# A decoder layer on one core: the mixing written out in set order, weight sums of two leading pairs made earlier, half of the embedding moved beside the first norm

## The chip, the cores and the metric

The kernel runs on one core of one Trainium2 chip. The time is device microseconds of one execution; the kernel before has 2464.32 us as the median of three (2461.43 to 2470.61). TensorE does the matmuls, VectorE (DVE in rows) and ScalarE (ACT) the elementwise work, GpSimd (POOL) the sums of weights, SyncE (SP) issues the transfers. In the trace a matmul's row covers its way through the pipeline; two rows that follow each other start closer together than one is long.

## The reference

One layer and the last norm, for 1024 tokens of width 1024, all in float32:

```
x += 0.5 * (silu(h @ w1) * (h @ w3)) @ w2,  h = rms(x)              # FFN1, inner width 2816
h  = rms(x); q, f, v, og, pool, ga, gb = split(h @ w_in)
f  = lb + (1 - lb) * sigmoid(f);  k = 1 - f;  q = silu(q)            # 8 heads of 128
S_t = diag(f_t) S_{t-1} + k_t outer v_t;  o_t = S_t^T q_t            # chunkwise
y_a = (rms(o) * onorm * silu(og)) @ w_branch_a
y_b = ((trailing means of pool over 2, 4, 8, 16 tokens - token) @ pool_w * scale) @ w_branch_b
x += (sigmoid(ga) * y_a + sigmoid(gb) * y_b) @ w_out
x += 0.5 * SwiGLU_2(rms(x))                                          # FFN2
x += sigmoid(rms(x) @ W_gate) * rms(p @ W_ple);  out = rms(x)
```

## The kernel before, in words

**Products.** Every float32 operand is split into a high and a low part, and each product is three matmuls of 128x128 by 128x512 (`mm3`, lines 150 to 152). The projections run in *pairs*: two blocks of 128 weight columns and the two token halves make a 2x2 product in seven multiplications instead of eight (`pair`), 12 matmuls each, 84 for a pair. For them, sums of the weights (S1 to S4) are made on GpSimd (lines 90 and 93), cast to their high parts on ScalarE (118), and the low parts taken on VectorE (119); sums of the activations (T1 to T3, N4) are made once in each norm.

**A norm's start.** Before FFN1, the mixing and FFN2 the first token half is normed and transposed (`first`), then the second half (`second`): TensorE scales and turns a block (L242), VectorE and ScalarE make the sums and their parts for blocks 0 to 3 (`act_second`, lines 191 to 193). Products 1 and 2 of a pair need the first half alone, so three *leading pairs* run these beside `second`; their weight sums are made later. Their further products wait for each of the four blocks in turn: T1's high part is `xT1h`.

**The mixing.** For each of 8 heads and 2 token halves `hgrn` does: diagonal scores (L810), transposes of v (L817), seven levels of scores (L837; each is followed by a masked copy on VectorE, L840, and a multiply of q and k, L87, that the next level's matmuls need), then the state (L863, L867), the output (L885, L887), a norm of it on ScalarE, GpSimd and VectorE (L892), and transposes of the result (L898) that are multiplied with the gate og (L899) and stored. A list `others` holds ten pairs (gates, pool branch); after each head's two halves the program text takes one or two, beside the next head's q and f pair. Where instructions stand on each engine is decided by a scheduler that goes by the text's order as priority.

**Around it.** The pool branch (`pool_group`) makes trailing means on VectorE in doubling steps, in two 512-wide buffers a step. After the heads come `branch_b` (8 column blocks, 24 matmuls each), `branch_a`, `w_out` in token-major form (`tok`), FFN2, the gate of the per-layer embedding (again `tok`) and the last norm. SBUF is in five tag pools: "a" 28, "w" 12 and "q" 4 buffers of 1024 columns, "u" 8 and "h" 5 of 512; PSUM has banks pA (3), pB (1), pC (1), aux (3). Transfers are all issued from one queue of SyncE in the order in which they stand there.

Of the kernel before, what the change touches and what calls it, by code (L numbers as in the profile page):

```python
# [16 lines left out]
P = 128  # L17
# [20 lines left out]
def hybrid_block(ctx: ExitStack, tc: tile.TileContext, a: dict, out: bass.AP):  # L38
# [208 lines left out]
    def norm_act(x, which, tr="aux"):  # L247
# [20 lines left out]
        def second():  # L268
            ts = range(4, 8)
            diag = scales(x, ts)  # L270
            yield
            for kc in range(0, KC, 2):
                p12 = turned_by(x, ts, diag, kc)
# [5 lines left out]
                yield  # L279
# [9 lines left out]

    def flush():  # L290
        while waiting:
            waiting.pop(0)()

    def pair(wa, wb, act, tiles, on11, on22, on21, on12, early=False):
# [6 lines left out]
        def product(i, ps, start):  # L301
            s, b = SIDES[i]
            hi, lo = w[s]
            for k in range(4):
                c = slice(k * P, (k + 1) * P)
                mm3(ps, hi[:, c], lo[:, c], *act[b][k], start and k == 0, k == 3)

# [13 lines left out]
        ra = raw(wa, "ra")  # L321
        if not early:
            rb = raw(wb, "rb")
        w["A11"], w["A12"] = halves(hilo(ra, "w", "wa"))
        if not early:
            sums(ra, rb)
        yield
# [6 lines left out]
        yield  # L334
        if early:
            sums(raw(wa, "ra"), raw(wb, "rb"))
        yield
        flush()
        pb = bank("pB")
        product(6, pa, False)  # L340
        nc.scalar.copy(c2, pa)  # L341
        product(5, pb, True)
        product(7, pa, False)
# [4 lines left out]
        def rest():  # L348
            product(4, pa, False)
            on21(pa)  # L350
            product(3, pb, False)
# [5 lines left out]
    def steps(it, n=9):  # L357
        for _ in range(n):
            if next(it, 0) == 0:
# [5 lines left out]
    def run_pair(*args, **kw):  # L365
        if not starts:
            steps(pair(*args, **kw))
            return

        second, n = starts[0], len(leads)  # L370
        it = pair(*args, **kw, early=True)
        leads.append(it)
        steps(it, 1 if n == 1 else 2)
        if n == 1:

            steps(leads[0], 1)
# [44 lines left out]
    def ffn_up(act, w1, w3, gs, after=None):  # L421
        chunk = []

        def one(c):
# [13 lines left out]
            run_pair(  # L438
# [748 lines left out]
```

## Time and profile before

| what | value |
|---|---|
| median of three (range) | 2464.32 us (2461.43 to 2470.61) |
| the profiled execution's own time, span of its trace | 2467.48 us, 2465.8 us |
| TensorE busy | 2346.3 us (95%), 11003 instructions |
| VectorE / ScalarE / GpSimd busy | 1482.6 (60%) / 975.2 (40%) / 446.4 us (18%) |
| mean granted clock of TensorE over the span | 0.979 |
| transfers | 334.10 MB, mean 135 GB/s |

The share of busy time is a mean over stages with different limits; the granted clock is told as a share of full speed.

### The profile page before, as it was taken

What the parts mean: (1) busy time and instruction counts of PE and PEld (TensorE: products, weight loads), DVE (VectorE), ACT (ScalarE), POOL (GpSimd) and SP (SyncE); (2) the same over time, 40 slices, a digit from 0 to 9 for tenths busy, and PEclk for the clock granted to TensorE, in tenths of its full rate; (3) what the DMA queues carried; (4) which work ended last, traced back from release to release, by engine and by line L of the source; (5) the groups of instructions that cost most, each with busy time, mean ns of one, the idle gap of its engine ahead of it and who ended that gap; (6) DMA issues with size and microseconds to landing.
All of it is one profiled execution on the core that took longest, in us unless ns stands there. A gap on an engine that the chain in (4) does not pass through costs nothing.

```text
span 2465.8 us, 29423 instructions
## 1 busy us (share of the span) xinstructions
PE 2346.3 (95%) x11003; PEld 1919.4 (78%) x11003; DVE 1482.6 (60%) x2026; ACT 975.2 (40%) x1511; POOL 446.4 (18%) x390
## 2 busy tenths in 40 slices
PE   8899999999998999989999989999899999999997
PEld 5688788888877778768778767777688888888885
DVE  5745555468565665684564675676645544568558
ACT  7433333333554334243333331236433333334654
POOL 2222232100013112122212201201232222100000
PEclk9999999999999999999999988999999999999998
DMA  5244554574232213122312346663225433663323
GB/s 205 88 160 140 176 179 139 177 277 141 90 121 76 90 48 120 56 98 74 107 59 79 117 149 209 221 219 129 98 90 175 154 124 112 211 246 124 109 101 133
DMA packets 133951, 334.10 MB, mean 135 GB/s; under 512 B 15280, under 2 KB 15792, under 8 KB 133808
## 3 DMA queue, kind: packets, MB, share of 16 engines
q1 hardware_dynamic: 133808, 332.23, 39.1%
q8 instruction: 86, 1.41, 0.2%
q14 instruction: 57, 0.47, 0.1%
HBM read 230.98 MB, written 101.19 MB: 135 GB/s over the span
## 4 chain that ended last, share of the span: by engine, by line
PE 80%; DVE 9%; ACT 3%; issue 3%; POOL 2%; DMA 2%; SPq 0%; DVEq 0%; POOLq 0%; ACTq 0%
PE pA L150 12%; PE pA L151 12%; PE pA L152 12%; PE pB L151 6%; PE pB L150 6%; PE pB L152 6%; PE aux L837 4%; PE pC L151 3%; PE pC L152 3%; PE pC L150 3%; PE aux L151 2%; PE aux L152 2%; PE aux L150 2%; DVE qk L87 1%; DVE tot L87 1%
## 5 line engine op out<-in xcount | busy, mean ns | idle before, releaser
L90 POOL TENSOR_TENSOR s<-rb 128x512 f32<-128x512 f32 x74 | 102.4, 1384 | 736.2 <-PE pA L152 359.7
L119 DVE TENSOR_TENSOR wtl<-rb,wth 128x1024 fp32r<-128x1024 f32 x74 | 90.7, 1225 | 152.2 <-ACT wth L118 151.8
L118 ACT CAST wsh<-s 128x1024 fp32r<-128x1024 f32 x74 | 77.8, 1051 | 231.0 <-POOL s L93 219.5
L93 POOL TENSOR_TENSOR rb<-ra,s 128x512 f32<-128x512 f32 x74 | 96.4, 1303 | 382.0 <-DVE wd L119 382.0
L837 PEld LDWEIGHTS aux<-qk 128*128 128x128 f32 (+1 forms) x896 | 107.2, 189 | 44.8 <-issue 28.2
L118 ACT CAST wth<-rb 128x1024 fp32r<-128x1024 f32 x74 | 77.6, 1048 | 155.4 <-POOL rb L93 155.4
L118 ACT CAST gh<-gr 128x1024 fp32r<-128x1024 f32 x84 | 81.8, 980 | 135.8 <-PE aux L151 86.4
L118 ACT CAST wah<-ra 128x1024 fp32r<-128x1024 f32 x74 | 77.9, 1052 | 134.9 <-PE pC L151 81.3
L837 PE MATMUL aux<-qk 128*128 128x64 f32 (+1 forms) x896 | 114.5, 272 | 17.4 <-DVE qk L87 16.5
L119 DVE TENSOR_TENSOR gl<-gr,gh 128x1024 fp32r<-128x1024 f32 x84 | 94.8, 1132 | 59.8 <-ACT gh L118 59.7
L150 PE MATMUL pA<-xT1h,wsh 128*128 128x512 f32 x280 | 111.9, 400 | 19.8 <-ACT xT1h L118 19.8
L119 DVE TENSOR_TENSOR wsl<-s,wsh 128x1024 fp32r<-128x1024 f32 x74 | 91.0, 1230 | 61.8 <-ACT wsh L118 50.4
L150 PE MATMUL pA<-xT3h,wth 128*128 128x512 f32 x296 | 118.1, 399 | 4.2 <-ACT g L341 3.2
L150 PE MATMUL pB<-xT1h,wsh 128*128 128x512 f32 x296 | 117.1, 396 | 1.8 <-ACT xT1h L118 0.9
L150 PE MATMUL pC<-x0h,wah 128*128 128x512 f32 x296 | 117.0, 395 | 1.5 <-ACT x0h L118 1.3
L152 PE MATMUL pA<-x0h,wal 128*128 128x512 f32 x296 | 116.7, 394 | 1.6 <-DVE wal L119 1.6
L152 PE MATMUL pB<-xT1h,wsl 128*128 128x512 f32 x296 | 117.9, 398 | 0.0
L151 PE MATMUL pC<-x0l,wah 128*128 128x512 f32 x296 | 116.8, 394 | 1.0 <-DVE x0l L119 1.0
L151 PE MATMUL pB<-xT1l,wsh 128*128 128x512 f32 x296 | 117.0, 395 | 0.4 <-DVE xT1l L119 0.4
L150 PE MATMUL pA<-x0h,wah 128*128 128x512 f32 x296 | 117.2, 396 | 0.0
L151 PE MATMUL pA<-xT3l,wth 128*128 128x512 f32 x296 | 117.0, 395 | 0.0
L152 PE MATMUL pA<-xT3h,wtl 128*128 128x512 f32 x296 | 117.0, 395 | 0.0
(338 smaller groups left out, 6580.6 us busy)
## 6 DMA issues: line engine op xcount, KB each, us to landing
ra<-in_ffn_w_dram SPq DMA_DIRECT2D x50, 512.0 KB, 3.7
rb<-in_ffn_w_dram SPq DMA_DIRECT2D x44, 512.0 KB, 4.0
gsS<-gs SPq DMA_DIRECT2D x88, 256.0 KB, 2.1
rB<-in_ffn_w_dram SPq DMA_DIRECT2D x40, 512.0 KB, 6.7
gr<-gsS SPq DMA_DIRECT2D x40, 512.0 KB, 3.5
gsA<-g SPq DMA_DIRECT2D x66, 256.0 KB, 2.0
gr<-gsA SPq DMA_DIRECT2D x30, 512.0 KB, 5.1
ra<-in_w_in_dram SPq DMA_DIRECT2D x29, 512.0 KB, 3.6
```

Source lines behind the costliest of these rows:

```text
L87: nc.vector.tensor_tensor(o, x, y, ALU.mult)
L90: nc.gpsimd.tensor_tensor(o, x, y, ALU.add)
L93: nc.gpsimd.tensor_tensor(o, x, y, ALU.subtract)
L118: nc.scalar.copy(hi, src)
L119: nc.vector.tensor_tensor(lo, src, hi.bitcast(F32), ALU.subtract)
L150: nc.tensor.matmul(ps, ah, bh, start=first, stop=False, **kw)
L151: nc.tensor.matmul(ps, ah, bl, start=False, stop=False, **kw)
L152: nc.tensor.matmul(ps, al, bh, start=False, stop=last, **kw)
L837: nc.tensor.matmul(ps[:m, c, :64], kc[c][:, :m], right, start=True, stop=True)
```

## The change

- **Mixing.** The eight heads are written under a manual schedule for TensorE: `head` runs a head's two halves in groups of matmuls (a `yield` behind each), and `among` deals the parts of other pairs (three matmuls, then a `yield False`) between the groups. A table `more` says which pairs stand beside which head; heads 1, 3 and 5 have the next v, qf and og pairs. Head 7 gets the last two gate pairs and the first block of `branch_b`.
- **Moved.** The transposes of the result, the gate multiply and the store (`turn`) stand two groups into the next half head. v is loaded ahead, og late. The pool means stand beside the next qf pair's parts, in "w" buffers; their maps follow.
- **Pairs.** The first result is copied from pC and pA added to it (it was the other way around). The weights' A parts of leading pairs go to spare "a" buffers, and the first two leading pairs have their sums made ahead of `second`; the third as before. In the mixing the leading pairs are v(0), qf(0), og(0).
- **FFN1's start.** Half of the embedding's product runs inside `second` (before blocks 0 and 2), its copies out of PSUM on ScalarE; raw weights of two leading pairs are loaded first.
- **Rest.** Order of some loads (`behind`), gb and o buffers; the last two items of the closing `tok` are one, so that its last four banks get twelve matmuls in a row each.

```diff
     def pair(wa, wb, act, tiles, on11, on22, on21, on12, lead=False, late=False,
...
-        w["A11"], w["A12"] = halves(hilo(ra, "w", "wa"))
-        if not early:
-            sums(ra, rb)
-        yield
+        w["A11"], w["A12"] = halves(hilo(ra, "a" if lead else "w", "wa"))
+        yield True
+        if not late:
+            sums(ra, raws[1] or raw(wb, "rb"))
+        yield True
         pa, pc = bank("pA"), bank("pC")
-        product(1, pa, True)
-        nc.scalar.copy(c1, pa)
-        product(2, pc, True)
-        add(c1, c1, pc)
+        yield from product(1, pa, True)
+        yield from product(2, pc, True)
+        nc.scalar.copy(c1, pc)
+        add(c1, c1, pa)
...
     def run_pair(*args, raws=(None, None), **kw):
...
+        second = starts.pop()
+        for it in leads:
             steps(it, 1)
+        steps(leads[0], 2)
+        steps(leads[1], 1)
+        steps(second, 2)
+        steps(leads[1], 1)
+        steps(second, 1)
+        steps(leads[2], 2)
         steps(second)
...
+            while means and next(means[0], 0) == 0:
+                means.pop(0)
...
+            both = t_("w", "pw")
+            nxt = [both[:, L], both[:, R]]
...
+        def turn():
+            ps = bank("aux")
+            for p_, a_ in zip(chunks(ps), qc):
+                nc.tensor.transpose(p_, a_, ident)
+            nc.vector.scalar_tensor_tensor(og, ps, onorm[:, h : h + 1], og, ALU.mult, ALU.mult)
+            store(o_dram[h][half], og)
...
+    GROUPS = 2 * 13
...
+            for i, _ in enumerate(hgrn(h, half)):
+                if i == 2 and turns:
+                    turns.pop(0)()
...
+        for i, _ in enumerate(groups, 1):
+            while done * GROUPS < i * n:
+                next(parts, None)
+                done += 1
...
+    more = {
+        0: lambda: (pool_pair(0), beside_means(qf_pair(1)), pool_maps(),
+                    gate_pair(GB, 0, gb_dram)),
+        2: lambda: (pool_pair(2), beside_means(qf_pair(3)), pool_maps(),
+                    gate_pair(GB, 2, gb_dram)),
+        4: lambda: (qf_pair(5), gate_pair(GB, 4, gb_dram), gate_pair(GB, 6, gb_dram)),
+        6: lambda: (qf_pair(7), gate_pair(GA, 0, ga_dram), gate_pair(GA, 2, ga_dram)),
+        7: lambda: around(gate_pair(GA, 4, ga_dram), act_b(), gate_pair(GA, 6, ga_dram), flushed(),
+                          branch_b(0)),
+    }
...
+            among(its, head(h), (74 if h == 7 else 3 * PAIR + 4 * (h in (0, 2))))
...
-    tok([(i, q) for i in ORDER for q in range(2)],
+    tok([(i, q) for i in ORDER for q in range(2)][:-2] + [(4, (0, 1))],
```

The order on TensorE in the second half of head 7, before (L898 turns the first half's result, L810, L817 and L837 are this half's groups, L150 to L152 a pair's matmuls):

```order
L898 MATMUL aux_10647<-ident,qk_9791 128x128 x4
L810 MATMUL aux_10659<-qk_9792 128x128 x4
L817 MATMUL aux_10665<-ident,v_10655 128x128 x4
L837 MATMUL aux_10680<-qk_9792 128x64 x4
L837 MATMUL aux_10687<-qk_9792 128x64 x4
L837 MATMUL aux_10694<-qk_9792 128x64 x4
L837 MATMUL aux_10701<-qk_9792 128x64 x4
L837 MATMUL aux_10708<-qk_9792 128x64 x4
L150 MATMUL pC_11381<-x0h_11226,wah_11360 128x512
L837 MATMUL aux_10715<-qk_9792 128x64 x4
```

The same place in the changed kernel, whose levels are line 898 (157 to 159 are `mm3`'s):

```order
L898 MATMUL aux_10821<-qk_9771 128x64 x4
L157 MATMUL pA_10651<-xT3h_5582,wth_10647 128x512
L158 MATMUL pA_10651<-xT3l_5583,wth_10647 128x512
L159 MATMUL pA_10651<-xT3h_5582,wtl_10648 128x512
L157 MATMUL pA_10651<-xT3h_5641,wth_10647 128x512
L158 MATMUL pA_10651<-xT3l_5642,wth_10647 128x512
L159 MATMUL pA_10651<-xT3h_5641,wtl_10648 128x512
L157 MATMUL pA_10651<-xT3h_5702,wth_10647 128x512
L158 MATMUL pA_10651<-xT3l_5703,wth_10647 128x512
L159 MATMUL pA_10651<-xT3h_5702,wtl_10648 128x512
L898 MATMUL aux_10837<-qk_9771 128x64 x4
```

Where seven levels stood with hardly a matmul between them, nine matmuls of a gate pair now stand between two levels, as in the other heads.

The order on VectorE before, in the pool branch of one group (pw and o are its means and tokens; no head's instruction stands among these):

```order
L758 SCALAR_TENSOR_TENSOR o_7766<-pw_7948,o_7766 128x496
L84 TENSOR_TENSOR o_7766<-pw_7948,o_7766 128x16
L758 SCALAR_TENSOR_TENSOR o_7765<-pw_7949,o_7765 128x512
L81 TENSOR_TENSOR pw_7989<-o_7763 128x511
L119 TENSOR_TENSOR pb_7958<-o_7766,pb_7958 128x512
L119 TENSOR_TENSOR pb_7967<-o_7765,pb_7967 128x512
L749 COPY pw_7989<-o_7763 128x1
L81 TENSOR_TENSOR pw_7990<-o_7764 128x511
```

In the changed kernel the later steps of one group stand between two levels of head 2: ahead of these rows is the multiply of one level, the last row is the next level's masked copy (L902):

```order
L81 TENSOR_TENSOR pw_7670<-pw_7652 128x508
L81 TENSOR_TENSOR pw_7670<-pw_7652 128x4
L87 TENSOR_TENSOR pw_7670<-pw_7670,invc 128x8
L802 SCALAR_TENSOR_TENSOR o_7233<-pw_7670,o_7233 128x504
L84 TENSOR_TENSOR o_7233<-pw_7670,o_7233 128x8
L802 SCALAR_TENSOR_TENSOR o_7234<-pw_7670,o_7234 128x512
L81 TENSOR_TENSOR f_7437<-f_7437,pB_7575 128x512
L119 TENSOR_TENSOR pwhl_7688<-pwr_7686,pwhl_7688 128x512
L119 TENSOR_TENSOR pb_7691<-o_7236,pb_7691 128x512
L718 TENSOR_SCALAR f_7437<-f_7437,lb_126,lb 128x512
L119 TENSOR_TENSOR pb_7700<-o_7235,pb_7700 128x512
L902 COPY_PREDICATED score_5422<-mask_81,aux_7665 128x64x4
```

A step of the means, the multiplies that end it and the low parts for the map now stand in VectorE's queue between one level's multiply and the next level's copy; before, they stood beside other work, in one piece.

The order on GpSimd at FFN2's start, before: the four powers of the norm of tokens 4 to 7 (L231), then the weight sums of a first and a second pair (L90, L93):

```order
L231 TENSOR_TENSOR rs_12722<-rs_12722,mhalf 128x1
L231 TENSOR_TENSOR rs_12731<-rs_12731,mhalf 128x1
L231 TENSOR_TENSOR rs_12740<-rs_12740,mhalf 128x1
L231 TENSOR_TENSOR rs_12749<-rs_12749,mhalf 128x1
L90 TENSOR_TENSOR s_2254_12704<-rb_12702 128x512
L93 TENSOR_TENSOR s_2254_12704<-s_2254_12704,ra_12700 128x512
L93 TENSOR_TENSOR rb_12702<-ra_12700,rb_12702 128x512
L93 TENSOR_TENSOR rb_12702<-ra_12700,s_2254_12704 128x512
L90 TENSOR_TENSOR s_2329_12987<-rb_12985 128x512
L93 TENSOR_TENSOR s_2329_12987<-s_2329_12987,ra_12983 128x512
```

In the changed kernel (the powers are L238):

```order
L93 TENSOR_TENSOR rb_12637<-ra_12619,rb_12637 128x512
L93 TENSOR_TENSOR rb_12637<-ra_12619,s_2212_12639 128x512
L238 TENSOR_TENSOR rs_12704<-rs_12704,mhalf 128x1
L238 TENSOR_TENSOR rs_12713<-rs_12713,mhalf 128x1
L90 TENSOR_TENSOR s_2221_12686<-rb_12684 128x512
L93 TENSOR_TENSOR s_2221_12686<-s_2221_12686,ra_12625 128x512
L93 TENSOR_TENSOR rb_12684<-ra_12625,rb_12684 128x512
L238 TENSOR_TENSOR rs_12722<-rs_12722,mhalf 128x1
L93 TENSOR_TENSOR rb_12684<-ra_12625,s_2221_12686 128x512
L238 TENSOR_TENSOR rs_12731<-rs_12731,mhalf 128x1
L90 TENSOR_TENSOR s_2292_13029<-rb_13027 128x512
```

The sums of two leading pairs now stand among and ahead of the powers, those of the third behind them.

## Rows read from the trace of the kernel before

**Rows 1.** The page: the span, and busy time of two engines

```profile
span 2465.8 us, 29423 instructions
PE 2346.3 (95%) x11003; PEld 1919.4 (78%) x11003; DVE 1482.6 (60%) x2026; ACT 975.2 (40%) x1511; POOL 446.4 (18%) x390
```

**Rows 2.** The view by windows, TensorE: stretch, length, busy (count), granted clock, DMA

```profile
450.00:500.00 50.00, 50.00 (x222) 1.00 0.63 222
800.00:1450.00 650.00, 615.49 (x3357) 1.00 0.27 89
1450.00:1500.00 50.00, 35.55 (x163) 0.66 0.36 117
1456.00:1494.00 38.00, 24.03 (x107) 0.59 0.30 98
1700.00:1750.00 50.00, 39.43 (x179) 0.86 0.29 106
2450.00:2465.80 15.80, 2.58 (x12) 0.70 0.36 133
```

**Rows 3.** TensorE's waits: us in total, times, longest

```profile
PE pA L150 <- ACT xT1h L118: 19.8, 5, 5.9
PE aux L837 <- DVE qk L87: 16.5, 17, 1.4
PE aux L898 <- DVE qk L892: 15.6, 11, 3.5
```

**Rows 4.** Timeline of a level, second half of head 1: start, us, what, idle before

```profile
907.62 1.02 PE L837 MATMUL aux<-qk 128*128 128x64 f32 x8
908.45 0.48 PE L150 MATMUL pC<-x0h,wah 128*128 128x512 f32 x1
908.67 0.44 DVE L840 COPY_PREDICATED score<-mask,aux 128x256 f32<-128x256 uint16 x1 [1.26 <-PE aux L837]
909.01 0.68 DVE L87 TENSOR_TENSOR qk<-qk,tot 128x512 f32<-128x512 f32 x1
909.92 1.00 PE L837 MATMUL aux<-qk 128*128 128x64 f32 x8
```

**Rows 5.** Timeline, a GpSimd sum, a multiply on VectorE, and the level behind them

```profile
884.16 1.47 POOL L93 TENSOR_TENSOR rb<-ra,rb 128x512 f32<-128x512 f32 x1
884.40 1.77 DVE L87 TENSOR_TENSOR qk<-qk,tot 128x512 f32<-128x512 f32 x1
886.23 0.68 PE L837 MATMUL aux<-qk 128*64 128x64 f32 x8 [0.95 <-DVE qk L87]
```

**Rows 6.** Timeline of TensorE, a level in head 7's second half

```profile
1471.87 1.94 PE L837 MATMUL aux<-qk 128*128 128x64 f32 x8 [1.21 <-DVE qk L87]
```

**Rows 7.** Timeline of VectorE inside a group of the pool branch

```profile
1066.13 0.68 DVE L81 TENSOR_TENSOR pw<-o 128x511 f32<-128x511 f32 x1
1066.80 0.68 DVE L81 TENSOR_TENSOR pw<-pw 128x510 f32<-128x510 f32 x1
```

**Rows 8.** The page's costliest groups: a weight's low part on VectorE

```profile
L119 DVE TENSOR_TENSOR wtl<-rb,wth 128x1024 fp32r<-128x1024 f32 x74 | 90.7, 1225 | 152.2 <-ACT wth L118 151.8
```

**Rows 9.** Timeline of the second feed-forward's start: VectorE and TensorE

```profile
1721.09 0.74 DVE L191 SCALAR_TENSOR_TENSOR t<-tr,gains,b 128x512 f32<-128x512 f32 x1
1741.78 1.75 DVE L119 TENSOR_TENSOR x<-b,x 128x512 fp32r<-128x512 f32 x1
1743.45 2.47 DVE L84 TENSOR_TENSOR t<-b,t 128x512 f32<-128x512 f32 x2
1746.33 0.79 PE L150 MATMUL pA<-xT1h,wsh 128*128 128x512 f32 x1 [4.56 <-ACT xT1h L118]
```

**Rows 10.** Timeline of the end: the last matmul, and VectorE behind it

```profile
2452.20 0.39 PE L152 MATMUL pB<-woh,yl 128*128 128x512 f32 x1
2457.40 2.74 DVE L1100 SCALAR_TENSOR_TENSOR x<-x,rs,gain 128x512 f32<-128x512 f32 x4 [0.47 <-POOL rs L162]
2461.13 1.42 DVE L1100 SCALAR_TENSOR_TENSOR x<-x,rs,gain 128x512 f32<-128x512 f32 x2 [0.73 <-POOL rs L162]
```

More of the change, by code (lines that the diff above doesn't have):

```diff
@@ L288, in hybrid_block, with flushed, pair @@
     waiting = []
+    def flushed():
+        while waiting:
+            yield from waiting.pop(0)()
     def flush():
-        while waiting:
-            waiting.pop(0)()
-    def pair(wa, wb, act, tiles, on11, on22, on21, on12, early=False):
+        for _ in flushed():
+            pass
+    def pair(wa, wb, act, tiles, on11, on22, on21, on12, lead=False, late=False,
+             raws=(None, None)):
         c1, c2, c3 = tiles
@@ L357, in steps @@
     def steps(it, n=9):
-        for _ in range(n):
-            if next(it, 0) == 0:
+        for end in it:
+            n -= end
+            if not n:
                 return
@@ L598, in hybrid_block, with embed @@
     e_ss = small("e_ss", [P, NT, 2])
-    def embed(half, ps_):
-        for t in range(4 * half, 4 * half + 4):
+    def embed(ts, ps_, banks):
+        for t in ts:
             c = slice((t % 4) * P, (t % 4 + 1) * P)
             for d in range(2):
-                ps = bank(("pA", "pB")[d])
+                ps = bank(banks[d])
                 for k in range(2):
@@ L713, in done @@
             store(v_dram[h + i][half], t)
-        out_pair(w_in[V + h], w_in[V + h + 1], act, done)
+            v_there.add((h + i, half))
+        yield from out_pair(w_in[V + h], w_in[V + h + 1], act, done)
+    og_there, og_last = set(), [None]
     def og_pair(h):
@@ L726, in done @@
             store(og_dram[h + i][half], t)
-        out_pair(w_in[OG + h], w_in[OG + h + 1], act, done)
+            og_there.add((h + i, half))
+        yield from out_pair(w_in[OG + h], w_in[OG + h + 1], act, done)
     def gate_pair(at, j, dst):
@@ L733, in done, with beside_means, pool_means @@
             store(dst[j + i][half], t)
-        out_pair(w_in[at + j], w_in[at + j + 1], act, done)
-    pw_split = []
-    def pool_group(g, u):
+        yield from out_pair(w_in[at + j], w_in[at + j + 1], act, done)
+    means, pooled = [], []
+    def beside_means(it):
+        for part in it:
+            yield part
+            while means and next(means[0], 0) == 0:
+                means.pop(0)
+        while means:
+            for _ in means.pop(0):
+                pass
+    def pool_means(g, u):
         win = 2 << g
@@ new lines, in among, with around @@
+    def among(its, groups, n):
+        parts = (p for it in its for p in it if not p)
+        done = 0
+        for i, _ in enumerate(groups, 1):
+            while done * GROUPS < i * n:
+                next(parts, None)
+                done += 1
+        for _ in parts:
+            pass
+    PAIR = 28
+    def around(first, acts, *its):
+        yield first
+        next(acts)
+        for it in its[:-1]:
+            yield it
+        next(acts)
+        yield its[-1]
+    more = {
[8 more added lines that the diff above has]
+    }
@@ L934, in branch_b, with act_b @@
+    for it in (v_pair(0), qf_pair(0), og_pair(0)):
+        steps(it)
+    m_parts = []
+    def act_b():
+        behind[0] = latest[0]
+        for g in range(NG):
+            m = t_("q", "m")
+            for half, c in enumerate((L, R)):
+                load(m[:, c], m_dram[g][half])
+            m_parts.append(halves(hilo(m, "a", "m")))
+        m_last, behind[0] = latest[0], None
+        yield True
+        behind[0] = m_last
+        yield True
     def branch_b(j):
@@ L943, in branch_b @@
                 mm3(ps, wh[:, c], wl[:, c], *m_parts[g][half], i == 0, i == 3)
-            t = t_("u", "o")
-            mul(t, ps, gb)
-            store(yb_dram[j][half], t)
+                yield False
+            mul(gb, ps, gb)
+            store(yb_dram[j][half], gb)
+    with tc.manual_schedule(engines={nc.tensor.engine}):
+        for h in range(HEADS):
+            its = more[h]() if h in more else (v_pair(h + 1), qf_pair(h + 1), og_pair(h + 1))
+            among(its, head(h), (74 if h == 7 else 3 * PAIR + 4 * (h in (0, 2))))
+        turns.pop(0)()
+    behind[0] = og_last[0]
     act_a = new_act()
@@ L970, in load_act @@
         put(("T3", "T2"), hilo(b2, "a", "xT3"))
-    for j in range(KC):
-        branch_b(j)
+    for j in range(1, KC):
+        steps(branch_b(j))
         if j % 2:
             load_act(j // 2)
+    behind[0] = latest[0]
     for j in range(0, KC, 2):
```

206 lines of the change are left out of this document (104 added, 102 removed).

## The prediction

> **What bounds it now.** I read the page first: TensorE is busy 2346.3 of 2465.8 us [rows 1], so 119.5 us without a matmul is all that waits can give back, beside what a low clock costs; the number of TensorE instructions hardly changes. The windows say where it lies. In FFN1 a stretch of 50 us is busy 50.00 at a granted clock of 1.00, with 222 matmuls: 0.225 us each, nothing to win there [rows 2]. The seven heads from 800 to 1450 us lose 650 − 615.49 = 34.5 us, the next 50 us lose 14.45, FFN2's start (1700 to 1750) 10.6, the end 15.8 − 2.58 = 13.2 [rows 2]. The waits name the releasers: T1's high part at the starts of the norms 19.8 us in 5 waits, the levels' multiply 16.5 in 17, the output's norm 15.6 in 11 [rows 3]. Then I read single levels. One of head 1: matmuls at 907.62, the masked copy at 908.67, the multiply at 909.01 for 0.68, the next level at 909.92; between the levels lie six pair matmuls from 908.45 on [rows 4]. The multiply is done at 909.69, so this chain wants about 1.2 us behind a level, and six matmuls (1.35 us) just hide it.
>
> **Mixing, the loss of before.** The heads' idle time is 34.5 + 14.45 = 49 us. [...] At full clock those 24.03 us would be about 24.03 × 0.59, which is 9.9 less. Loss in all: 59 us.
>
> **Mixing, what the set order leaves.** The order puts 84 parts and more (74 in head 7), three matmuls each, between 26 groups: nine or twelve matmuls, 9 × 0.225 = 2.03 us at least, behind each group. Against the 1.2 us that a level's chain wants, 0.8 us are spare. Four terms remain.
> - *Levels that are late all the same.* Of the 17 waits on the multiply about five, near 1.2 us each, are head 7's [rows 3, 6]; the other twelve hold 10.5 us, 0.87 each. Three more matmuls than the six of rows 4 cover 0.68 of it at most, a low part of 1.225 us ahead in the queue [rows 8] still shows: I leave 0.4 each, 5 us. Bounds: 0 and the 10.5 of now.
> - *Pool means.* In a chain, a long VectorE step and a short one together take 1066.80 − 1066.13 = 0.67 us [rows 7], so 0.60 and 0.07. In head 2 the copy of level 4 stands behind nine long and four short operations: 5.7 us, and with its own copy and multiply (about 1.0, [rows 4]) 6.7, where TensorE has 0.8 + 2.03 = 2.85 us of work: 3.8 us late. The level before it has four long and four short ones ahead (2.7 + 1.0): 0.85 late; the neighbours add 0.9. Head 0, whose windows are 2 and 4, has about half: 2.5. Together 8; bounds 0 (VectorE is ahead when they come) and 16 (each stretched as in rows 5).
> - *The clock.* The gaps of before cost no clock from 800 to 1450 (1.00, [rows 2]); a stop of 3.8 us among shorter ones may: 2 us, between 0 and 10.
> - *Starts of pairs, late loads, the first groups of a head*: 4 us, between 0 and 10. Weights keep 12 buffers, but the means take some of them in heads 0 and 2; when they are late, the next pair's parts stop the heads too, since TensorE's order is fixed.
>
> 19 us remain, the gain is 59 − 19 = **40 us**. The wait for the output's norm (15.6) goes into this: its transposes now stand behind two groups of the next half, some 5 us of other work, against a longest wait of 3.5 [rows 3]. If that cover fails, it is 3.5 × 16 at most. The final one, after head 7, stands alone ahead of `branch_b`; in its place the result's way to `branch_a` has seven blocks of 24 matmuls, 37.8 us, ahead of it, so it costs nothing.
>
> **FFN2's start.** Three leading pairs run ahead of the four blocks; the last block's T1 arrives at 1746.33 after 4.56 us of idle time [rows 9]. From the first block (1721.09) it takes 25 us. Two of VectorE's operations near the end are stretched, to 1.75 and to 2.47 for two [rows 9], against 0.68 each for a plain one [rows 4]: 2.2 us lost while GpSimd made sums. Those of two pairs now come ahead of it, and one low part of a weight (1.225, [rows 8]) falls out of the chain: 3.4 us. Twelve plus nine matmuls, 2.0 us more per start in all, can be done before the last block. Against it, two powers of the norm now stand behind three and four sums; the diagonal was ready some 10 us before it was used, so I take no loss. Gain **5**, bounds −4 (the sums push the first block) and 8 (all of the idle time but 2.6).
>
> **The mixing's and FFN1's start.** The same edits, but in the mixing one weight load stands behind three stores of x, which takes the gain back: 0, bounds −3 and 3. In FFN1 half the embedding (48 matmuls, 10.8 us) moves from ahead of `second` to beside it; eight copies go to ScalarE, which makes T1's high part; at 0.68 each as for VectorE [rows 4] they can hold it back 5.4 us, and the cover is worth at most its wait, 5.9 [rows 3]. I take 0, −5 to +5.
>
> **The end.** The last matmul is issued at 2452.20 and VectorE still works at 2461.13 + 1.42 [rows 10]: the last four banks become ready 1.35 us apart (six matmuls), and each needs some 3 us of VectorE. With twelve matmuls they are 2.7 us apart, so three of four tiles are done when the last comes: two operations of 0.68, the norm's, two of 0.71 and a store remain, some 8.5 us of 13.2. Gain **4.5**, 3 to 6. c1's copy and add only trade banks; nothing.
>
> **Sum.** 40 + 5 + 0 + 4.5 = 49.5 us. 2467.48 − 49.5 = 2418; the profiled execution is 3.2 above the median of 2464.32, so the median would be 2415. I forecast **2416 us**, 2.0% less.
>
> [...] What stretches VectorE can be seen: a GpSimd sum begins at 884.16, a multiply at 884.40 takes 1.77 us instead of 0.68, and the level waits 0.95 [rows 5]. [...]
>
> **Rivals.**
> 1. *All of it is covered* (chance 0.22). VectorE runs ahead, the means cost 1, late levels 2, nothing else: 4 us remain, the gain is 55 + 9.5. 2400.
> 2. *Pool heads stop for weights* (0.18). Means hold "w" buffers, so ra and rb of the next pair come late, in heads 0 and 2: a stop of some 8 us and a half clock behind it for 10 us each, (8 + 5) × 2 = 26 more. 2441. For it: the order is fixed; against: a pair now stretches over 8 groups and leaves its loads more time.
> 3. *Sums meet multiplies* (0.09). 23 pairs in the heads, four sums each, 92: were each to stretch one multiply by 1.09, less the 0.8 spare, plus a masked copy stretched alike, about 0.5 us a time, 46 us, 41 more than in the sum. 2457: no change. Against: GpSimd is busy 18% [rows 1].
> 4. *Slower: every level waits* (0.05). VectorE takes its queue in order. If ahead of each level's copy stands an operation that itself waits for the pair's next product, all 112 chains (16 half heads, seven each) stop by s: 2416 + 112 s. From s = 0.43 nothing is gained; at 0.8, one low part and a half of what it waits for, 2505.
> 5. *Only the waits' places change* (0.04): head 7's cover is taken from the other heads, starts and end give nothing: 2462.
>
> The forecast's own case has 0.42, from 2407 to 2428. Rivals 1 and 2 with it hold 0.82: the range is 2398 to 2450. About 0.5% (12 us) is what a measurement can tell from no change: faster takes in the forecast and rivals 1 and 2, 0.83; rivals 3 and 5 make 0.11 with the edge; slower 0.06.
>
> **What would show it.** Right: head 7 at a granted clock of 1.00 and no wait of L969 on VectorE; the heads' windows above 96% busy; waits of L898 on the multiply, few outside heads 0 and 2, the longest (about 4 us) in head 2; last block of FFN2 some 4 us nearer to its first; last store 8 to 9 us behind the last matmul. Wrong: clock dips in heads 0 and 2, TensorE waiting for a pair's parts or for v or og, multiplies of 1.8 us at most levels, or T1 later at the starts.

## The result, and the profile after

The changed kernel takes 2427.82 us, median of four (2423.76 to 2433.22), beside 2463.81 of the kernel before on the same chip: a ratio of 0.9851, interval 0.9822 to 0.9879. It is 36 us faster; 2416 was forecast, in a range of 2398 to 2450.

The page of the profiled execution (2433.22 us):

```profile
span 2431.5 us, 29305 instructions
PE 2332.4 (96%) x11003; PEld 1915.3 (79%) x11003; DVE 1471.6 (61%) x2019; ACT 979.2 (40%) x1520; POOL 443.6 (18%) x390
```

Against [rows 1] TensorE has 14 us less busy time for as many instructions (in part less half clock: the mean granted clock is 0.986 instead of 0.979) and 20 us less idle time: 34.3 us of span. The view by windows for TensorE (stretch, length, busy and count, granted clock, DMA):

```profile
800.00:1400.00 600.00, 584.04 (x3225) 0.99 0.25 82
1400.00:1456.00 56.00, 50.36 (x266) 0.94 0.62 202
1418.00:1432.00 14.00, 12.30 (x56) 0.76 0.64 218
1000.00:1050.00 50.00, 46.58 (x232) 0.93 0.31 106
```

The heads now lose 16 of 600 us and 5.6 of 56, where 34.5 of 650 and 14.45 of 50 were lost [rows 2], and head 7 runs mostly at 1.00; half clock is left in three short places, near 890, 1013 and 1419 (granted clock 0.66 from 889 to 894, 0.57 from 1012 to 1020 and from 1418 to 1426). TensorE's waits (us in total, times, longest):

```profile
PE aux L898 <- DVE qk L87: 8.4, 13, 1.3
PE pA L157 <- ACT g L355: 7.0, 8, 1.7
PE aux L898 <- DVE tot L87: 4.2, 3, 1.4
PE aux L898 <- ACT wb L118: 3.1, 1, 3.1
PE aux L158 <- DVE pb L119: 2.4, 1, 2.4
PE aux L969 <- DVE qk L961: 0.6, 1, 0.6
```

The wait of the transposes on the output's norm, 15.6 us in 11 [rows 3], is 0.6 in one. The multiply holds the levels 8.4 us instead of 16.5. The copy out of pA behind product 6 (line 355) holds product 7 for 7.0 us in eight waits. Before, the same copy (line 341) held it in three:

```profile
PE pA L150 <- ACT g L341: 3.2, 3, 1.5
```

Those three were in FFN1. In FFN2 the wait is new, 4.7 us in four, and the forecast has no term for it.

Where the 34.3 us come from is told best by five marks that both traces have: the first matmul of FFN1's down projection (`w2h`), the first and the last of `w_out`, the first of FFN2's down projection, and the first of the embedding's gate. The stretches between are differences of the starts of those rows; the last goes to the span's end.

| stretch, us | before | after | difference | forecast |
|---|---|---|---|---|
| start, FFN1 up | 489.6 | 490.7 | +1.2 | 0 |
| FFN1 down, mixing, branches | 1117.9 | 1078.8 | −39.1 | −40 |
| w_out | 95.8 | 93.5 | −2.4 | 0 |
| FFN2's start and up | 438.3 | 444.3 | +6.0 | −5 |
| FFN2 down | 219.4 | 219.4 | 0.0 | 0 |
| gate and end | 104.8 | 104.8 | 0.0 | −4.5 |

Stretches with the same code scatter from trace to trace: in the traces of the experiments below w_out took 90.6 to 94.9 us, and in the six kernels that share the changed kernel's feed-forwards (it, tail_two_items, turn_in_place, head7_bare, two_parts_a_group, means_in_one_piece) FFN1 took 490.7 to 494.8, 492.8 on the mean, FFN2 up (its start and up projections) 439.8 to 444.3, 442.2 on the mean. Against the one trace of before, that is 3.2 and 3.9 us lost; w_out's difference says nothing. The gate and the end took 103.2 to 105.3 us in all the traces, and the mixing's stretch 1076.2 to 1078.8 in the three kernels that have the same code there (it, tail_two_items, rb_in_ffn).

TensorE over the whole stretch of the mixing, before and after:

```profile
489.60:1607.40 1117.80, 1057.81 (x5317) 0.98 0.35 120
490.70:1569.50 1078.80, 1043.08 (x5318) 0.99 0.37 123
```

Of the 39 us that it is shorter, 24.3 are idle time and 14.7 are busy time for the same matmuls.

### The profile page after: what moved, and what is told of

Its sections match the earlier page's. It is cut to its first block, busy times and chain, and to the rows that moved or that the text cites. A ratio compares the mean times of both kernels' runs of the same rounds, so it can differ in the third digit from the quotient of the medians.

```text
span 2431.5 us, 29305 instructions
## 1 busy us (share of the span) xinstructions
PE 2332.4 (96%) x11003; PEld 1915.3 (79%) x11003; DVE 1471.6 (61%) x2019; ACT 979.2 (40%) x1520; POOL 443.6 (18%) x390
## 4 chain that ended last, share of the span: by engine, by line
PE 71%; DVE 10%; DMA 7%; ACT 4%; POOL 3%; issue 3%; SPq 1%; POOLq 0%; DVEq 0%; ACTq 0%
PE pA L157 11%; PE pA L159 11%; PE pA L158 11%; PE pB L157 5%; PE pB L158 5%; PE pB L159 5%; PE aux L898 3%; PE pC L158 3%; PE pC L159 3%; PE pC L157 3%; PE aux L158 2%; PE aux L159 2%; PE aux L157 2%; DMA rb<-in_ffn_w_dram 1%; DVE qk L87 1%
## 5 line engine op out<-in xcount | busy, mean ns | idle before, releaser
L90 POOL TENSOR_TENSOR s<-rb 128x512 f32<-128x512 f32 x74 | 99.5, 1345 | 815.1 <-DMA rb<-in_ffn_w_dram 408.7
L119 DVE TENSOR_TENSOR wtl<-rb,wth 128x1024 fp32r<-128x1024 f32 x74 | 90.6, 1225 | 149.2 <-ACT wth L118 149.2
L93 POOL TENSOR_TENSOR rb<-ra,s 128x512 f32<-128x512 f32 x74 | 97.2, 1314 | 352.5 <-DVE wd L119 325.8
L119 DVE TENSOR_TENSOR wsl<-s,wsh 128x1024 fp32r<-128x1024 f32 x74 | 90.7, 1226 | 99.9 <-ACT wsh L118 99.9
L898 PEld LDWEIGHTS aux<-qk 128*128 128x128 f32 (+1 forms) x896 | 110.0, 187 | 37.9 <-issue 11.1
L119 DVE TENSOR_TENSOR wal<-ra,wah 128x1024 fp32r<-128x1024 f32 x74 | 91.4, 1237 | 78.5 <-PE pC L158 45.5
L157 PE MATMUL pA<-xT1h,wsh 128*128 128x512 f32 x280 | 115.2, 411 | 18.1 <-ACT xT1h L118 14.8
L898 PE MATMUL aux<-qk 128*128 128x64 f32 (+1 forms) x896 | 111.1, 267 | 17.1 <-DVE qk L87 8.4
L157 PE MATMUL pB<-x,wth 128*128 128x512 f32 x296 | 118.3, 400 | 0.0
L158 PE MATMUL pA<-x0l,wah 128*128 128x512 f32 x296 | 115.9, 392 | 0.8 <-DVE x0l L119 0.8
```

The costliest lines, as they stand in the source:

```text
L90: nc.gpsimd.tensor_tensor(o, x, y, ALU.add)
L93: nc.gpsimd.tensor_tensor(o, x, y, ALU.subtract)
L119: nc.vector.tensor_tensor(lo, src, hi.bitcast(F32), ALU.subtract)
L157: nc.tensor.matmul(ps, ah, bh, start=first, stop=False, **kw)
L158: nc.tensor.matmul(ps, ah, bl, start=False, stop=False, **kw)
L898: nc.tensor.matmul(ps[:m, c, :64], kc[c][:, :m], right, start=True, stop=True)
```

## The experiments

Twelve kernels ran, each an edit of the changed kernel. Medians are compared through the ratio to the kernel before on the same chip; stretches are those of the table, from one trace each.

| run | median, us | ratio (interval) | FFN1 | to w_out | FFN2 up |
|---|---|---|---|---|---|
| the changed kernel | 2427.82 | 0.9851 (0.9822 to 0.9879) | 490.7 | 1078.8 | 444.3 |
| rb_behind_ra | 2427.78 | 0.9842 (0.9822 to 0.9862) | 485.5 | 1083.7 | 437.6 |
| c1_from_pA | 2435.93 | 0.9883 (0.9865 to 0.9901) | 491.6 | 1075.7 | 444.8 |
| rb_and_c1 | 2430.50 | 0.9856 (0.9837 to 0.9876) | 487.7 | 1084.7 | 438.0 |
| tail_two_items | 2430.58 | 0.9855 (0.9835 to 0.9874) | 494.8 | 1076.7 | 443.1 |
| rb_in_ffn | 2418.47 | 0.9815 (0.9800 to 0.9829) | 487.9 | 1076.2 | 437.8 |
| leads_as_before | 2428.89 | 0.9855 (0.9840 to 0.9869) | 492.2 | 1081.0 | 441.2 |
| turn_in_place | 2443.10 | 0.9912 (0.9898 to 0.9927) | 492.4 | 1092.2 | 439.8 |
| head7_bare | 2466.71 | 1.0005 (0.9995 to 1.0015) | 493.1 | 1112.1 | 442.8 |
| two_parts_a_group | 2469.16 | 1.0013 (0.9999 to 1.0027) | 492.4 | 1114.1 | 440.1 |
| means_in_one_piece | 2436.16 | 0.9880 (0.9849 to 0.9911) | 493.4 | 1079.8 | 443.2 |
| m_low_on_gpsimd | 2417.83 | 0.9803 (0.9777 to 0.9828) | 487.6 | 1074.6 | 438.1 |
| low_parts_on_gpsimd | 2416.34 | 0.9808 (0.9794 to 0.9821) | 487.6 | 1072.9 | 437.7 |

### Why FFN2 lost 6 us instead of winning 5

One of the four waits of FFN2 up, in the timeline of the changed kernel (SPq are SyncE's transfers as it issues them):

```profile
1816.32 0.42 SPq L149 DMA_DIRECT2D ra<-in_ffn_w_dram  x1
1822.69 1.04 SPq L153 DMA_DIRECT2D wgT<-qB  x2
1824.14 0.32 SPq L153 DMA_DIRECT2D wgN<-qB  x1
1824.55 0.40 SPq L149 DMA_DIRECT2D rb<-in_ffn_w_dram  x1
1828.36 1.28 POOL L90 TENSOR_TENSOR s<-rb 128x512 f32<-128x512 f32 x1 [12.35 <-DMA rb<-in_ffn_w_dram]
1828.83 0.39 PE L159 MATMUL pA<-xT1h,wsl 128*128 128x512 f32 x1
1831.04 1.05 ACT L118 CAST wsh<-s 128x1024 fp32r<-128x1024 f32 x1 [4.24 <-POOL s L93]
1832.52 0.57 ACT L355 COPY g<-pA 128x512 f32<-128x512 f32 x1
1833.14 0.50 PE L157 MATMUL pA<-xT3h,wth 128*128 128x512 f32 x1 [1.20 <-ACT g L355]
```

Read from the end: product 7 waits 1.20 us for the copy out of pA; that copy stands on ScalarE behind the cast `wsh`, which waits 4.24 us for GpSimd's sum, which waits 12.35 us for rb. rb was issued at 1824.55, 8.2 us after its ra, behind the four stores of a set of the gate's weight sums (the last three stand here). In the text of `pair`, rb's load had moved behind the cast of the A parts, and so behind these stores in SyncE's queue. The copy's last matmul had ended at 1829.22 (1828.83 + 0.39), but ScalarE, idle until 1831.04, did not take the copy ahead of the cast.

```diff
         ra = raws[0] or raw(wa, "ra")
+        rb = raws[1] or (None if lead else raw(wb, "rb"))
...
-            sums(ra, raws[1] or raw(wb, "rb"))
+            sums(ra, rb or raw(wb, "rb"))
```

> The raw rb block of every pair that leads nothing is loaded right behind ra again, ahead of the A parts. Theory 1 (FFN2 lost 6 us, from 438.3 to 444.3 between w_out's last matmul and the first of the down projection, because rb's load now stands behind four stores of weight sums in SyncE's queue, so GpSimd's sums and the cast wsh come late and ScalarE holds the copy out of pA): the four waits of product 7 for that copy in FFN2 (1.20, 1.74, 0.53, 1.25, sum 4.7) go, 444.3 becomes 439.5; in FFN1 some 2 us; the whole about 2421 against 2427.8. Rival (the loss is at FFN2's start, at half clock): the stretch stays at 444, the whole within 2 us.

FFN2 up took 437.6 us, FFN1 485.5: theory 1 holds. Over all traces the sizes are steadier: in the five kernels with rb behind ra FFN2 up took 437.6 to 438.1 and FFN1 485.5 to 487.9 (487.3 on the mean), 4.4 and 5.5 us less than the means above. But here the mixing's stretch grew by 4.9, and the median did not move. The other suspect was c1, whose sum now reads pA later:

```diff
-        yield from product(2, pc, True)
-        nc.scalar.copy(c1, pc)
-        add(c1, c1, pa)
+        nc.scalar.copy(c1, pa)
+        yield from product(2, pc, True)
+        add(c1, c1, pc)
```

> c1 is copied from pA right behind product 1 and pC added, as before the change; nothing else. Theory 2: product 6, which goes on in pA, waits for VectorE's add of pA into c1 where VectorE has a norm's or weight sums' work ahead (1.15, 1.12, 1.01 in FFN1): FFN1 3.3 us shorter, FFN2 unchanged at 444, the whole about 2424.5. Rival: these waits too come from late weight sums, then nothing changes (within 1 us in FFN1).

> Both edits together. If theories 1 and 2 hold and add up: 6 to 7 and 3.3 us, about 2418. If only the first holds: 2421.

Theory 2 falls: FFN1 took 491.6 us. The waits of product 6 on VectorE's add (3.3 us in three in the changed kernel) were gone, but the next product waited in their place, in c1_from_pA's waits of TensorE:

```profile
PE pA L157 <- ACT g L355: 10.6, 9, 3.1
```

7.0 us in eight had become 10.6 in nine. Nor did the two edits add up. What was late was rb, whichever copy of pA stood behind it. The medians with the old order of c1 are 8 us (c1_from_pA) and 3 us (rb_and_c1) above those without it, but the intervals of the ratios overlap both times, so it is not shown that the new order wins anything. Then the good half alone, rb behind ra where `ffn_up` calls `pair`:

```diff
+        rb = raws[1] or (raw(wb, "rb") if both and not lead else None)
...
-                raws=raws.get(c, (None, None)),
+                raws=raws.get(c, (None, None)), both=True,
```

> rb right behind ra in the feed-forwards' pairs only; the mixing and branch_a as in the changed kernel. In the run rb_behind_ra FFN1 took 485.5 us up to the first down matmul (490.7 in the changed kernel), FFN2's part 437.6 (444.3), but the mixing 862.4 (857.5). If the late rb load is the cause in FFN1 and FFN2 and the earlier one costs the mixing its 5 us: 486, 438 and 856 here, about 2417 in all, ratio 0.981. Rival (the mixing's 5 us are scatter between runs): 2420 to 2424.

2418.47 us, a ratio of 0.9815, 0.36% under the changed kernel's 0.9851; FFN2 up 437.8, the mixing back at 1076.2. The intervals of the two ratios still touch (0.9822 to 0.9829); the stretches do not: in FFN1 and in FFN2 each of the five kernels with rb behind ra is below each of the six with the late rb. The timeline of the same pair as above (SyncE, GpSimd), and TensorE's wait that is left:

```profile
1815.51 0.33 SPq L153 DMA_DIRECT2D wgT<-qT  x1
1815.88 0.43 SPq L149 DMA_DIRECT2D rb<-in_ffn_w_dram  x1
1821.08 1.28 POOL L90 TENSOR_TENSOR s<-rb 128x512 f32<-128x512 f32 x1 [10.11 <-DMA rb<-in_ffn_w_dram]
```

```profile
PE pA L157 <- ACT g L356: 1.5, 2, 1.0
```

rb is issued behind one store instead of four, and the waits for the copy are 1.5 us in two, from 7.0 in eight. Why an early rb costs the mixing some 5 us (1083.7 and 1084.7 against 1076 to 1079) stays open: in rb_behind_ra v's loads hold TensorE 3.6 us instead of 0.4, but no run takes that away.

### What the leading pairs' sums were worth

```diff
-        leads.append(pair(*args, **kw, lead=True, late=len(leads) == LEADS - 1, raws=raws))
+        leads.append(pair(*args, **kw, lead=True, late=True))
...
-        steps(leads[0], 2)
-        steps(leads[1], 1)
-        steps(second, 2)
-        steps(leads[1], 1)
-        steps(second, 1)
-        steps(leads[2], 2)
+        steps(leads[0], 3)
+        steps(leads[1], 1)
+        steps(leads[0], 1)
+        steps(second, 2)
+        steps(leads[1], 2)
+        steps(leads[2], 3)
```

> The sums of all three leading pairs are made late, in the order of before; the embedding still beside the first norm, the rest as changed. The forecast's step: FFN2's start loses 5 us again, the others nothing: about 2433. Rival, from the profile after (the last block's T1 comes 5.4 us later at the mixing's start, 0.8 later at FFN2's, 1.4 earlier at FFN1's, with 2 us more done before each): the earlier sums are worth nothing in all, 2428 within 2, and with late sums the mixing's T1 comes 4 to 5 us earlier, FFN2's within 1.

The edit also takes away the early loads of two leading pairs' raw weights in FFN1. 2428.89, a ratio of 0.9855 against 0.9851: nothing in all, the rival was right. (Its last guesses were not: the mixing's T1 came no earlier, FFN2's 3.5 us earlier.) FFN1 took 492.2, FFN2 up 441.2, both within the scatter. The place shows why, at FFN2's start in the changed kernel (GpSimd, VectorE, TensorE by start):

```profile
1680.09 1.30 POOL L93 TENSOR_TENSOR rb<-ra,s 128x512 f32<-128x512 f32 x1 [2.20 <-DVE rs L237]
1681.34 0.55 POOL L238 TENSOR_TENSOR rs<-rs,mhalf 128x1 f32<-128x1 f32 x1
1681.92 0.29 DVE L239 TENSOR_SCALAR diag<-ident,rs 128x128 f32<-128x128 f32 x1 [1.26 <-POOL rs L238]
1683.64 0.74 DVE L198 SCALAR_TENSOR_TENSOR t<-tr,gains,b 128x512 f32<-128x512 f32 x1
1706.82 0.79 PE L157 MATMUL pA<-xT1h,wsh 128*128 128x512 f32 x1 [2.07 <-ACT xT1h L118]
```

The first block's multiply comes 20.7 us behind w_out's last matmul (1662.94), where it came 17.8 behind it before (1703.26 to 1721.09, [rows 9]): the fourth power stands behind a sum on GpSimd, and the diagonal waits for it. From the first block to the last T1 it then takes 23.2 us instead of 25.2. The same two rows in leads_as_before, where w_out's last matmul is at 1663.78:

```profile
1678.60 0.75 DVE L198 SCALAR_TENSOR_TENSOR t<-tr,gains,b 128x512 f32<-128x512 f32 x1 [0.73 <-PE tr L249]
1704.17 0.80 PE L157 MATMUL pA<-xT1h,wsh 128*128 128x512 f32 x1 [2.42 <-ACT xT1h L118]
```

With late sums the first block comes 14.8 us behind w_out, 5.9 earlier, and from there to the last T1 it takes 25.6 us, 2.4 more. So the early sums cost 3.5 us at the last T1, for about 2 us of matmuls that can run before it. What the sums gave to the blocks, their place ahead of the powers more than took.

### What makes the mixing shorter

```diff
-            among(its, head(h), (74 if h == 7 else 3 * PAIR + 4 * (h in (0, 2))))
+            among(its, head(h), (0 if h == 7 else 3 * PAIR + 4 * (h in (0, 2))))
```

> Head 7's groups stand without any pair's matmuls between them; the two gate pairs and the first block of branch_b follow it. Forecast's step (head 7's loss of before was missing cover and the half clock that came with it): each half takes some 31 us for 13 us of work, 36 us more in all, 2464, with a granted clock of 0.5 to 0.6 through most of 60 us. Rival (the cover only moves the wait elsewhere): within 10 us of 2428.

2466.71, a ratio of 1.0005: as much as the whole change won. The window over its two halves, and one level:

```profile
1374.00:1424.00 50.00, 32.31 (x162) 0.58 0.07 21
```

```profile
1383.47 1.94 PE L898 MATMUL aux<-qk 128*128 128x64 f32 x8 [1.21 <-DVE qk L87]
```

17.7 us idle, and 32.31 us of work at 0.58: about 31 us lost in 50, where head 7 of before lost some 24 in 38 [rows 2, 6]. Both theories of cost (missing cover, and the half clock behind it) are seen; the rival is out.

```diff
-            among(its, head(h), (74 if h == 7 else 3 * PAIR + 4 * (h in (0, 2))))
+            among(its, head(h), 2 * GROUPS)
```

> Two parts (six matmuls, 1.35 us) behind every group instead of three or four; what is left of a head's pairs follows the head in one piece. Forecast's step (a level's chain wants 1.2 us, the three matmuls more cover 0.68 us of what is late): the waits on the multiply (8.4 us in 13 in the changed kernel) grow to some 15 to 25 us, the means' stops in heads 0 and 2 by 0.7 us a level, the whole to about 2440. Rival (operations of several us in VectorE's queue make a level late, whatever the cover): within 4 us of 2428.

2469.16, a ratio of 1.0013: 41 us, three times what the forecast's step gave. TensorE's wait and the heads' window:

```profile
PE aux L898 <- DVE qk L87: 33.9, 43, 3.4
```

```profile
800.00:1400.00 600.00, 559.76 (x3051) 1.00 0.24 79
```

43 levels wait, 0.79 us each, and the window has 24 us less of matmuls than in the changed kernel. So six matmuls do not nearly hide a level everywhere; the level that I took for all [rows 4] found VectorE free. Each of the two edits costs what the change won, so the gain is neither head 7's cover nor the nine matmuls alone. I read it so: every group needs enough beside it, and matmuls that are spent in bulk are missing elsewhere.

```diff
-        turns.append(turn)
+        turn()
```

> The transposes of a half head's result stand one group behind its output again, not two groups into the next half. The forecast's step (the wait on the output's norm, 15.6 us before, is taken away by the move): the norm wants about 4 us from the output's matmuls, one group covers 2.0, so some 2 us for each of 16: 2427.8 + 30, with waits of L969 on VectorE's L961. Rival (other work in ScalarE's and VectorE's queues, not the place, sets it): under 10 us.

15.3 us slower, 2443.10: half of what was expected, but no rival's "under 10". The wait is back in full,

```profile
PE aux L969 <- DVE qk L961: 26.7, 16, 2.1
```

and costs 13.4 us of the mixing's stretch. Part of it was won back at the levels. In the changed kernel they wait 8.4, 4.2 and 3.1 us for three releasers; here one of the three is left:

```profile
PE aux L898 <- DVE qk L87: 8.0, 12, 1.9
```

As a size for what the move is worth in this order, 13 to 15 us is near the 15.6 of before [rows 3].

### The pool means, and what is left in head 7

In the changed kernel three stops of head 2 answer to the term on pool means:

```profile
998.35 1.08 PE L898 MATMUL aux<-qk 128*128 128x64 f32 x8 [1.05 <-DVE qk L87]
1002.65 1.08 PE L898 MATMUL aux<-qk 128*128 128x64 f32 x8 [0.68 <-DVE qk L87]
1010.91 0.50 PE L158 MATMUL aux<-pb,pwhl 128*128 128x512 f32 x1 [2.38 <-DVE pb L119]
```

With two in head 0 (1.06 and 0.78) they make 5.95 us; 8 were forecast, one of 3.8 among them.

```diff
-                    means.append(pool_means(g + k, [got.pop((k, 0)), got.pop((k, 1))]))
+                    for _ in pool_means(g + k, [got.pop((k, 0)), got.pop((k, 1))]):
+                        pass
```

> The pool means are traced where the pair's results arrive, in one piece, not step by step beside the next pair's parts; the rest as changed. Forecast's step (what stands between two levels on VectorE sets the stop: 0.67 us for a long and a short operation): the same 40 operations stand between fewer levels, a group of 16 tokens' window has 6.5 us of them, so each of four stops 2 to 5 us longer, 8 us in all and a half clock behind it, about 2438. Rival (VectorE has slack before and behind): within 3 us of 2428.

The median is 8 us above, near what was expected, but the intervals of the two ratios overlap, so a difference is not shown; the profiled execution's mixing is only 1 us longer. What the trace does show is the mechanism: in head 2 one stop of 8.44 us where there were three of 4.1 in all (TensorE, VectorE).

```profile
1008.66 1.94 PE L899 MATMUL aux<-qk 128*128 128x64 f32 x8 [8.44 <-ACT pb L118]
1007.83 0.68 DVE L87 TENSOR_TENSOR qk<-qk,f 128x512 f32<-128x512 f32 x1
```

The profile names ScalarE's cast, which ends at 1008.56, but the multiply that the level reads ends at 1008.51, and it stands behind 12.7 us of work on VectorE without a break (from 995.10), nearly all of it the means.

What is left in head 7 is one wait, 3.06 us in the changed kernel and 3.41 in rb_in_ffn, followed by half clock (0.57 from 1418 to 1426 in the changed kernel; in rb_in_ffn 0.79 from 1414 to 1430, with a level of 1.94 us). In rb_in_ffn (TensorE, VectorE):

```profile
1415.71 1.94 PE L899 MATMUL aux<-qk 128*128 128x64 f32 x8 [3.41 <-DVE qk L87]
1413.74 1.23 DVE L119 TENSOR_TENSOR ml<-m,mh 128x1024 fp32r<-128x1024 f32 x1 [1.44 <-ACT mh L118]
```

```diff
-            m_parts.append(halves(hilo(m, "a", "m")))
+            mh, ml = t_("a", "mh", F32R), t_("a", "ml", F32R)
+            nc.scalar.copy(mh, m)
+            nc.gpsimd.tensor_tensor(ml, m, mh.bitcast(F32), ALU.subtract)
+            m_parts.append(halves((mh, ml)))
```

> As rb_in_ffn, and the low parts of the pooled blocks m in head 7 are made on GpSimd. In rb_in_ffn a level of head 7 waits 3.41 us at 1415.71 for a multiply that stands behind such a low part on VectorE, which waits for ScalarE's cast, which waits for m's transfer; the next levels run at half clock. Theory (VectorE's queue carries a late transfer into the level): the wait goes, and some 3 us of half clock: 2413 against 2418.5. Rival (ScalarE's casts and the transfers hold the level anyway): within 2 us.

2417.83, no change that can be told, and the wait was longer:

```profile
1413.91 1.04 DVE L119 TENSOR_TENSOR wb<-rw,wb 128x512 fp32r<-128x512 f32 x1 [4.79 <-ACT wb L118]
1416.84 1.94 PE L899 MATMUL aux<-qk 128*128 128x64 f32 x8 [4.17 <-DVE qk L87]
```

The next low part in VectorE's queue, of a block of branch_b's weights, had taken m's place. With those of the first three blocks on GpSimd as well:

```diff
+        if j < 3:
+            t = t_("w", "wb", F32R)
+            wh, wl = t[:, :HALF], t[:, HALF:]
+            nc.scalar.copy(wh, r)
+            nc.gpsimd.tensor_tensor(wl, r, wh.bitcast(F32), ALU.subtract)
+        else:
+            wh, wl = hilo_half(r, "w", "wb")
```

> As m_low_on_gpsimd, and the low parts of branch_b's first three weight blocks on GpSimd too. In m_low_on_gpsimd the level of head 7 waited 4.17 us all the same, at 1416.84: its multiply then stood behind the low part of such a weight block, for which VectorE had idled 4.79 us behind ScalarE's cast and the block's transfer. Theory (VectorE takes its queue in order, so any late transfer ahead of a multiply holds the level): now nothing late is left ahead, the wait of about 4 us and the half clock behind it (0.82 over 16 us, some 2.5 us) go: mixing 847 us against 853, the whole 2412 against 2417.8. Rival (ScalarE's queue, where casts wait for the same transfers, holds the head): mixing 852 to 854, no change in all.

The window of rb_in_ffn for TensorE, then that of this run, and rows of GpSimd and VectorE from its timeline:

```profile
1400.00:1456.00 56.00, 50.93 (x266) 0.94 0.70 225
```

```profile
1400.00:1456.00 56.00, 54.81 (x289) 1.00 0.79 260
```

```profile
1417.31 1.29 POOL L1049 TENSOR_TENSOR wb<-rw,wb 128x512 fp32r<-128x512 f32 x1 [0.43 <-ACT wb L1048]
1417.52 1.63 DVE L87 TENSOR_TENSOR qk<-qk,tot 128x512 f32<-128x512 f32 x1
```

Head 7's last 56 us are busy 54.81 instead of 50.93, at 1.00 instead of 0.94: the mechanism holds. The time followed less: the mixing's stretch took 1072.9 us against 1076.2, the median 2416.34 with a ratio of 0.9808 against 0.9815, which is no difference that these runs tell. It is the lowest median of all.

### The end

```diff
-    tok([(i, q) for i in ORDER for q in range(2)][:-2] + [(4, (0, 1))],
+    tok([(i, q) for i in ORDER for q in range(2)],
```

> The last two items of the closing token-major product are two again, six matmuls in a bank each. Forecast's step: 4.5 us slower. Rival, from the profile after (VectorE is busy 12.07 of the last 12.60 us before the last matmul): VectorE and not the matmuls' order sets the end, so the stretch from the gate's first matmul to the end stays at 104.8 us within 0.5.

Gate and end took 104.8 us again, where the kernels with the changed order took 103.2 to 105.3; 4.5 us are not there, and the rival was right. The end of the changed kernel: the windows for VectorE before and behind the last matmul, then a row of VectorE and one of ScalarE.

```profile
2404.00:2416.60 12.60, 12.07 (x23) 1.00 0.49 163
2416.60:2431.50 14.90, 8.95 (x21) 0.59 0.38 141
```

```profile
2414.72 1.89 DVE L81 TENSOR_TENSOR x<-x,g 128x512 f32<-128x512 f32 x3
2417.29 0.57 ACT L1202 ACTIVATE g<-pA 128x512 f32<-128x512 f32 x1
```

VectorE has 12.07 us of work in the last 12.60. The third bank's matmuls end near 2413.9, but its sigmoid (L1202) runs at 2417.29, since ScalarE has squares ahead of it that wait for VectorE's adds (L81).

## Why the prediction was right, and where its steps were off

In the two traces 34.3 us were won where 49.5 were forecast. The 15 that are missing are FFN2's start (11) and the end (4.5); the mixing gave what was forecast of it.

- *Mixing*, 40 us forecast: 39.1 measured, and by the cause that it named. Head 7's idle time and half clock are gone; head7_bare brings them back and with them the whole time of before. The forecast's 9.9 us for the clock are worked out from 24.03 us at 0.59 [rows 2]; in head7_bare it was 32.31 us at 0.58. Left in the heads are 16 + 5.6 us of idle time and some 6 for the clock (24% of 12.3 us and 7% of 46.6), 28 where 19 were forecast: late levels about 10 (8.4 + 4.2, less 2.8 that belong to the means) instead of 5, means 6 instead of 8, the clock 6 instead of 2, and for late loads, pairs' starts and first groups 6 instead of 4, of which 3.1 are head 7's wait behind a late load.
- *Why 39.1 meets 40.* By these sizes 59 − 28 = 31 us would have been won; that the stretch is 39.1 shorter, and so meets the forecast, is in part luck. The other 8 are not idle time, since outside the heads TensorE idles no less than before (8.3 and 2.4 us from 700 to 800 and behind the heads, now 8.9 and 4.5): they are busy time, which fell by 14.7 us where the forecast counted 8 for the clock. What of it is clock and what is rows that a stop makes longer (0.50 us at 1010.91, 0.40 for the row behind it) I did not split.
- *The mixing's weak steps.* The weakest was to let one level's row stand for all: two_parts_a_group shows how much hangs on three matmuls more. The order was not quite as the sum has it either: 74 parts on 26 groups leave some groups of head 7 with six matmuls. And the clock of 1.00 from 800 to 1450 [rows 2] was a mean: behind a wait of 2.49 us at 1058.36 it is 0.79 from 1058 to 1066.
- *Signs.* The heads' windows are 97% busy up to 1400 us, as forecast, and 90% in head 7's last 56, at a clock of 0.94, not 1.00. The last block of FFN2 is 2 us nearer to its first, not 4. Nine of the 13 waits on the multiply are outside heads 0 and 2, though few were to be; the longest stop of head 2 is 2.38 us, not 4. The span ends 14.9 us behind the last matmul, not 8 to 9.
- *The output's norm* was forecast to go behind two groups' work: its wait fell from 15.6 to 0.6 us, and in place costs 13 to 15.
- *FFN2's start*, 5 us forecast to be won, 6 lost in the table's trace and 3.9 on the mean of six. Two steps failed. "The diagonal was ready some 10 us before it was used, so I take no loss": with sums ahead of the powers, it is the diagonal that is waited for; that takes the gain back. And the sum has no term for where rb's load goes in SyncE's queue, though the edit moved it behind the A parts: that cost FFN2 4.4 us and FFN1 5.5. These 10 us are rb_in_ffn's gain (9.4 by the medians). With rb behind ra FFN2 takes 437.8 us, 0.5 less than before: that is what the rest of the change is worth there.
- *Start and FFN1*, 0 forecast: 3.2 lost on the mean of six, with the late rb's 5.5 in it; so the start itself won some 2 us, against the one trace of before. The early raw weights and sums give nothing that can be told (492.2 without them in leads_as_before, 492.8 with them). No run puts the embedding back, so what its move is worth is not shown.
- *The end*, 4.5 forecast, 0 measured. "Three of four tiles are done when the last comes" took VectorE to have only those tiles; it was busy 12.07 of the last 12.60 us before the last matmul, so banks that come earlier find it busy.
- *Rivals.* Late loads did stop a head (rival 2), but head 7, for 3 us, not heads 0 and 2, and the first of them is a pooled block m; a weight block holds the level when m is out of the way (m_low_on_gpsimd). Stretched multiplies (rival 3) are seen, but not at most sums: 21 of the heads' 128 multiplies of q and k take over 0.9 us, 13 before. Rival 4's point, 0.43 us a level, is nearly what two_parts_a_group has: 33.9 us over 112 levels is 0.30, and its time is that of before; that pairs' products are what its levels wait for, as rival 4 has it, is not shown. Its premise on VectorE's order is seen in the trace of before: VectorE idles 2.34 us ahead of a low part at 191.70 and only then takes the multiply behind it at 192.84, whose last matmul had ended at 188.56.

## What to carry to other kernels

A chain of short dependent steps beside dense work is worth covering by count: find how many matmuls hide one step when the other engines are as busy as they are on the mean, not in the best row. When a load moves in the program text, look where it lands in its queue and which stores stand ahead of it. And before more is made ready earlier for an engine, look whether that engine is already busy.

## What the hardware showed that was not expected

Stops of 3.41 us (rb_in_ffn, 1415.71) and 4.17 (m_low_on_gpsimd, 1416.84) were followed by a level of 1.94 us, where one in head 1 of before took 1.02 [rows 4], and by a clock of 0.79 (from 1414 to 1430) and 0.82 (from 1416 to 1432). But a single wait of 1.43 us, in head 1 of the changed kernel, was also followed by a lower clock (0.66 from 889 to 894):

```profile
889.15 1.12 PE L898 MATMUL aux<-qk 128*128 128x64 f32 x8 [1.43 <-DVE tot L87]
```

Two waits of 1.36 us in the same kernel (1063.86 and 1227.85) were not (1.00 from 1060 to 1070 and from 1226 to 1232). And two_parts_a_group lost 40 of its 600 us, over half of it in waits of 1.1 to 1.3, at a granted clock of 1.00 over the window; its stop of 3.36 us was followed by a lower clock (0.91 from 875 to 895). In head7_bare, where waits of 1.2 us stand before levels with hardly a matmul between, the clock is 0.58. So the length of one stop does not tell by itself what the clock does; these runs do not separate more.

Beside work given to GpSimd a multiply on VectorE took longer. In the run low_parts_on_gpsimd a low part on GpSimd begins at 1417.31 and takes 1.29 us; the multiply that VectorE begins at 1417.52 takes 1.63 us, where it takes 0.68 in [rows 4], and ends 0.55 us behind the low part. In [rows 5] the multiply of 1.77 us ends 0.54 us behind GpSimd's sum. Why the multiply takes longer there is not shown.
